# Pair plans of gate_up and down: four pairs in the last group, ten pairs in the second pass

## The chip, the core and the metric

The kernel runs on one core of one Trainium2 chip. The time is device microseconds of one execution. The kernel before takes 1428.76 us, the median of three runs (1428.35 to 1428.78).

## The reference

One layer of an encoder with a sequence of 256 rows, model width 2048 and a feed-forward width of 5632, all in float32:

```python
for l in range(DEPTH):
    h = rms_norm(x, norm_g[l, 0])
    ...
    x = x + mix @ w_out[l]
    x = x + cross_attention(rms_norm(x, norm_g[l, 1]), mem_n, w_xq[l], w_xkv[l], w_xo[l])
    x = x + swiglu(rms_norm(x, norm_g[l, 2]), w_gate_up[l], w_down[l])
return rms_norm(x, final_norm_g)

def swiglu(h, w_gate_up, w_down):
    gate, up = jnp.split(h @ w_gate_up, 2, axis=-1)
    return (jax.nn.silu(gate) * up) @ w_down
```

The change concerns only swiglu: the product with w_gate_up (2048 x 11264) and the product with w_down (5632 x 2048).

## The kernel before

**Split precision.** Each float32 operand is kept as two parts, hi and lo. ScalarE casts the weight (`wh`), VectorE subtracts (`wl = raw - wh`). A product of a 128-wide activation tile with a weight of 512 columns is three matmuls (`part`, L472 to L474): hi with wh, hi with wl, lo with wh.

**The weight stream.** The weights lie in DRAM in the order of their use, in slabs of 128 x 2048 (1 MB). `_load` fetches a slab into a raw buffer on SP's queue. `_plain` and `_sums` split its parts into a ring of wh/wl buffers; a part is split only when the ring has room, some three to four parts ahead of TensorE. There are three raw buffers, and a fourth one (`rx`) during gate_up; the ring loses one place (`wz`) and the fourth raw buffer within the last gate_up group, where `begin` calls `back`.

**Plain slabs and pairs.** A slab holds four blocks of 512 columns, for two tiles of the inner dimension and two column groups. In a plain slab (`N` in a plan) each block meets both row halves: 8 products, 24 matmuls, two parts of 1024 columns. A pair slab computes the same 2 x 2 x 2 block product with seven products (a scheme of the Strassen-Winograd kind), 21 matmuls. It uses sums of weight blocks and sums of activations. Its four parts are: products 1 and b0 (1024 columns), a0 (512), 5 and 7 (1024), 6 and a1 (1024). The sums of weights are either made by VectorE, with four adds of 512 columns, or partly by DMA: then a spare tile `t` (one of the residual buffers `res`) is filled with one block on SP's queue, ScalarE copies it, and GpSimd's queue adds two more blocks by an accumulating DMA; VectorE then makes only two adds, and the third part is split from `t`. Slabs of that kind are in `SUMMED`, and `_load` starts their sums three slabs ahead (`AHEAD`).

**Activations of a pair.** `combine` forms the sums of two activation tiles on VectorE and ScalarE: two adds of 256, four of 128, and the splits of the results into a `y` tile (`z` in gate_up) and, for a last quarter called x4, back into the first activation tile. The generator `combined` runs it, driven by a background queue and forced by `before` when a pair needs it. Each pass of down reuses the combined tiles that the pass before has made.

**Order.** gate_up has a first plain group and ten paired groups of eight slabs, nine with the plan `NSSNSSNN` and the last with `NSNSNSNN`. Its results go transposed through DRAM (`hidden`) and come back through `fetch` into the activation tiles f[0] to f[43]: f[20] to f[27] lie in the tiles `z` that hold gate_up's combined activations, f[28] to f[43] in those of gate_up's input. Down then runs in two passes of 22 slabs, each for 1024 output columns, with 6 pairs in the first pass and 9 in the second; the last 12 steps of the second pass are held back for `down_end`. In `paired_rows` the products go to PSUM banks: a0, a1, b0, b1 of the plain slabs to one pool of four (`pg` in the first pass of down, `pm` in the second), 1, 6, 7 and 5 of the pairs to the other. `mixed` and `done` add them to the residual when a pass is through its pairs, or through all; so the second pass's 1, 6, 7, 5 take, in this order, the banks that a0, a1, b0, b1 of the first pass had. The residual was stored to DRAM before gate_up and is read back after it into `res`.

The order on an engine follows the order of the program's list within gate_up and down (`last` in `_half`, `keep_place`) for splits and fetches, and a planner's placing for the rest.

Of the kernel before, what the change touches and what calls it, by code (L numbers as in the profile page):

```python
# [19 lines left out]
ALU = mybir.AluOpType  # L20
# [8 lines left out]
FT = DFF // P  # L29
# [10 lines left out]
ROWS = ((0, 512), (704, 1024), (1088, NBLK))  # L40

LATE = 12

GATE_UP = 1920 // 16 + 8
GROUPS = *["NSSNSSNN"] * 9, "NSNSNSNN"

DOWN = GATE_UP + 80
PASSES = "NNNNNSNNSNNSNSNNSNNSNN", "NSNSNSNSNSNSNSNSNSNNNN"

PAIRED = {a + i for a, plan in [(GATE_UP + 8 * j, GROUPS[j % len(GROUPS)]) for j in range(10)] + [(DOWN, PASSES[0]), (DOWN + 22, PASSES[1])]  # L50
          for i, x in enumerate(plan) if x in "Ss"}
AHEAD = (-3, -3)

SUMS = [{GATE_UP + 8 * j + i + a: GATE_UP + 8 * j + i for j in range(10) for i, x in enumerate(GROUPS[j % len(GROUPS)]) if x == "S"}
        for a in AHEAD]

SUMMED = {GATE_UP + 8 * j + i for j in range(10) for i, x in enumerate(GROUPS[j % len(GROUPS)]) if x == "S"}

LAG, OWED, SOON, FAR = 1.3, 0.9, 0.01, 18.0
V_NG = 0  # L60
# [16 lines left out]
class Stream:  # L77


    def __init__(self, tc, pools, W, bg):  # L80
        self.tc, self.nc, self.W, self.bg = tc, tc.nc, W, bg
        self.rawp, self.wp = pools
        self.order = []
        self.n = self.made = 0
        self.after = []
        self.halves = []
        self.at = self.phase = 0
        self.raw = None
        self.ring = [[self.wp, -1] for _ in range(3)]
        self.last = {}  # L90
        self.raws = [[self.rawp, -1] for _ in range(3)]
        self.sums = []
        self.places = []
        self.two = []
        self.begun = []

    def _buffers(self, n, m):

# [6 lines left out]
    def _load(self, n):  # L105

        nc = self.nc
        slot = min(self.raws, key=lambda x: x[1])
        slot[1] = n
        self.raw = slot[0].tile([P, 2048], F32, name="raw", tag="raw")  # L110
        if n // 16 in SUMS[0]:
            t = self.sums[0]
            self.sums.append(self.sums.pop(0))
            nc.sync.dma_start(t[:, 0:512], self.W[SUMS[0][n // 16]][:, 1536:2048])
            self.begun.append(t)
        if n // 16 in SUMS[1]:
            t = self.begun.pop(0)
            mark = len(nc.cur_bb.bb.instructions)
            nc.scalar.copy(t[:, 512:1024], t[:, 0:512])  # L119
            self.keep(mark)  # L120
            nc.gpsimd.dma_start(t, self.W[SUMS[1][n // 16]][:, 512:1536], accum_op=ALU.add)  # L121
            self.two.append(t)
        if n // 16 in SUMMED:
            nc.sync.dma_start(self.raw[:, 0:1536], self.W[n // 16][:, 0:1536])
            return
        for a, b in zip(CUTS[n], CUTS[n][1:]) if n in CUTS else [(0, 1024), (1024, 2048)] if self.after else [(0, 2048)]:
            (nc.scalar if (n, a) == (0, 0) else nc.sync).dma_start(self.raw[:, a:b], self.W[n // 16][:, a:b])
            if self.after:
                self.after.pop(0)()

    def _half(self):
# [161 lines left out]
class Block:  # L293
# [563 lines left out]
    def whole(self, c):  # L857
        return self.res[c].rearrange("p k r -> p (k r)")

    def leave(self, c):  # L860
        self.nc.sync.dma_start(self.rd[:, c * 1024:(c + 1) * 1024], self.whole(c))

# [237 lines left out]
    def gate_up(self, gp, f, z):  # L1100

        nc = self.nc
        box, g, stored = {}, {}, []
# [36 lines left out]
        def fetch(k0, k1, ahead, pause, after=0, slow=False):  # L1140

            m = {}
            for k in range(k0, k1 + ahead):
                if k < k1:
                    while len(stored) <= k // 4:
                        yield
                    while after and self.bg.now < stored[k // 4] + after:
                        yield
                    m[k] = self.tmp()
                    mark = self.mark()  # L1150
                    self.load_turned(m[k], self.ff, k)
                    self.keep_place(mark)
                    if slow and k < k0 + ahead - 1:
                        yield
                if k >= k0 + ahead:
                    while k0 == 0 and k - ahead >= 20 and "free" not in box:
                        yield
                    mark = self.mark()
                    self.split(f[k - ahead], m.pop(k - ahead))
                    self.keep_place(mark)  # L1160
                    self.have = k - ahead + 1
                    yield pause
# [41 lines left out]
        self.st.raws.append([rx, -1])  # L1204
        gate(ps[0])
        up(0, ps[1])
        early = fetch(0, FT - 22, 2, 2.0, 12, True)
        self.bg.drain(comb)
        for j in range(1, DFF // 512):
            plan = GROUPS[(j - 1) % len(GROUPS)]  # L1210
            if j == 10:
                box["free"] = True
            turns = [i for i, x in enumerate(plan) if x == "N"][:3]
            if j == 10:
                rest = fetch(FT - 22, FT, 6, SOON, slow=True)

            def begin(i):

                if (j, i) == (10, 5):
                    self.st.back(self.wz, rx)  # L1220
                if i in turns:
                    next(early, None)
                if j == 10 and i > 2:
                    next(rest)

            upped(j, self.paired_rows("w_gate_up", [j * 512, DFF + j * 512], self.h3, sums[:8 - plan.count("N")], plan, mixed, gated,
                                      before=begin, swap=j % 2 == 0)[0])
        more.close()
        for c, x in enumerate(whole):
            nc.sync.dma_start(x, self.rd[:, c * 1024:(c + 1) * 1024])  # L1230
        for _ in early:
            pass
        self.fetch = self.bg.add(rest)
# [1 line left out]
    def down(self, f, sp):  # L1235
# [4 lines left out]
        nc, st = self.nc, self.st  # L1240
        ss = self.rp.tile([P, 24], F32, name="rc", tag="rc")
        self.gap(sp, 192)
        z = [sp.tile([P, 768], F32R, name=f"y{i}") for i in range(8)]
        u = sp.tile([P, 512], F32, name="u")
        sums = [((2 * i, 2 * i + 1), z[i % 8]) for i in range(PASSES[1].count("S"))]
        made, split = [], []

        def combined(n):
            for ks, x in sums[len(made):n]:
                yield from self.combine(x, *(f[k] for k in ks))  # L1250
                made.append(x)
                yield 2.0
# [32 lines left out]
        asked = itertools.count(1)  # L1285

        def ready(k):

            need = min(FT, max(k + 3, FT - 22 + next(asked) * 3 // 4))
            while self.have < need:  # L1290
                self.bg.step(next(e for e in self.bg.q if e[0] is self.fetch))

        for i, plan in enumerate(PASSES):
            n = plan.count("S")
            g = self.bg.add(combined(n))
            late = (0, LATE)[i]
            plan = plan[:22 - late // 4]

            def before(j):
                while plan[j] == "S" and len(made) <= plan[:j].count("S"):  # L1300
                    self.bg.step(next(e for e in self.bg.q if e[0] is g))
                if late and j == len(plan) - 2:
                    st.back(self.wy)

            ps, rest = self.paired_rows("w_down", [2 * i * 512, (2 * i + 1) * 512], f, sums[:n], plan,
                                        lambda *q: mixed(2 * i, *q), lambda *q: done(2 * i, *q), ready, late, before, i == 1,
                                        () if i else range(2 * n, 2 * n + 8))
            if i == 0:
                done(1, *ps)
        return ss, ps, rest, split  # L1310
# [316 lines left out]
class Gla:  # L1627
# [364 lines left out]
```

## Time and profile before

| what | value |
|---|---|
| median of three runs | 1428.76 us |
| the profiled execution | 1428.43 us |
| its span, first to last instruction | 1426.6 us |
| ScalarE busy | 850.2 us (60%) |
| GpSimd busy | 243.4 us (17%) |
| HBM read / written | 321.07 MB / 22.54 MB |
| DMA queue of the hardware (q1), share of 16 engines | 57.4% |
| DMA queue of the software (q0, GpSimd) | 17.2% |

In the lines of the profile PE is TensorE, PEld its weight loads, DVE VectorE, ACT ScalarE, POOL GpSimd and SP the queue that issues most DMAs. A timeline row has the start and the length in microseconds, engine, line of the code, operation, output<-inputs, shape and count; in brackets stands how long the engine was idle before it, and what ended the wait. Lengths of instructions on one engine can overlap, so the distance between starts is also needed. A row by windows gives for each engine the busy time and the number of instructions in a stretch.

### The profile page before, as it was taken

To read this page: it belongs to the slowest core of one execution; us is meant where nothing else is said; L and a number is where in the kernel's file an instruction comes from. 1 tells how busy PE (TensorE), PEld (TensorE's weight loads), DVE (VectorE), ACT (ScalarE), POOL (GpSimd) and SP (SyncE) were. 2 spreads that over 40 slices of the span, in tenths; PEclk is the share of its full clock that TensorE was granted. 3 is DMA by queue.
4 is the path that set the end of the run, shared out by engine and by line. 5 is a ranking of instruction groups with operands and counts; after the bars stand their busy time and mean duration, and the time that the engine had idled before them with its cause. 6 is when DMAs were issued, how large, how long until landed. Compare 5 with 4: busy or idle time off the path is not lost.

```text
span 1426.6 us, 18663 instructions
## 1 busy us (share of the span) xinstructions
PE 1416.5 (99%) x6562; PEld 1176.1 (82%) x6562; DVE 1174.3 (82%) x1782; ACT 850.2 (60%) x1242; POOL 243.4 (17%) x315
## 2 busy tenths in 40 slices
PE   9999999999999999999999999999999999999997
PEld 8888888888888888888888888888888888788886
DVE  6667868787878767677578999999999988989997
ACT  7566665445755555555465676667666665655655
POOL 0000100003212233531331121122211024000000
PEclk9999999999999999999999999999999999999999
DMA  9886554457566797965798999999999898665554
GB/s 356 294 291 250 204 198 174 161 177 232 183 216 215 234 278 249 276 197 188 252 298 257 265 280 283 288 291 260 278 291 273 276 276 242 212 235 179 193 220 148
DMA packets 72462, 344.84 MB, mean 242 GB/s; under 512 B 10894, under 2 KB 12591, under 8 KB 45745
## 3 DMA queue, kind: packets, MB, share of 16 engines
q1 hardware_dynamic: 52976, 285.31, 57.4%
q0 software_dynamic: 18960, 57.69, 17.2%
q8 instruction: 51, 0.84, 0.2%
q10 hardware_dynamic: 432, 0.66, 0.1%
q14 instruction: 43, 0.34, 0.1%
HBM read 321.07 MB, written 22.54 MB: 241 GB/s over the span
## 4 chain that ended last, share of the span: by engine, by line
PE 92%; issue 3%; DVE 2%; DMA 2%; POOL 1%; ACT 0%; SPq 0%; DVEq 0%; ACTq 0%; POOLq 0%
PE pg L472 21%; PE pg L474 21%; PE pg L473 21%; PE pm L473 6%; PE pm L474 6%; PE pm L472 6%; PE pg L420 4%; PE pg L421 2%; PE pm L1445 1%; DMA raw<-in_W 1%; PE pm L1074 1%; DMA tmp<-hidden 1%; POOL tmp L605 1%; PE pm L1045 1%; DVE wl L179 0%
## 5 line engine op out<-in xcount | busy, mean ns | idle before, releaser
L167 DVE TENSOR_TENSOR wl<-raw,wh 128x1024 fp32r<-128x1024 f32 (+1 forms) x395 | 473.7, 1212 | 161.3 <-ACT wh L166 159.4
L166 ACT CAST wh<-raw 128x1024 fp32r<-128x1024 f32 (+1 forms) x395 | 406.4, 1042 | 253.0 <-PE pg L474 189.0
L472 PE MATMUL pg<-wh,act 128*128 128x512 f32 (+1 forms) x1165 | 455.5, 391 | 0.0
L474 PE MATMUL pg<-wh,act 128*128 128x512 f32 (+1 forms) x1165 | 453.9, 390 | 0.5 <-DVE act L322 0.5
L473 PE MATMUL pg<-wl,act 128*128 128x512 f32 (+1 forms) x1165 | 453.6, 389 | 0.2 <-DVE wl L167 0.2
L474 PEld LDWEIGHTS pg<-wh,act 128*128 128x128 f32 x1165 | 218.9, 188 | 47.0 <-DVE act L322 1.1
L472 PEld LDWEIGHTS pg<-wh,act 128*128 128x128 f32 x1165 | 219.0, 188 | 46.8 <-issue 1.5
L473 PEld LDWEIGHTS pg<-wl,act 128*128 128x128 f32 x1165 | 219.0, 188 | 45.1 <-DVE wl L167 0.5
L178 ACT CAST wh<-raw 128x1024 fp32r<-128x1024 f32 (+1 forms) x177 | 161.5, 918 | 158.8 <-DVE raw L189 62.7
L179 DVE TENSOR_TENSOR wl<-raw,wh 128x1024 fp32r<-128x1024 f32 (+1 forms) x177 | 182.7, 1057 | 25.7 <-ACT wh L178 24.3
L473 PE MATMUL pm<-wl,act 128*128 128x512 f32 x290 | 112.9, 389 | 0.2 <-DVE wl L167 0.2
L472 PE MATMUL pm<-wh,act 128*128 128x512 f32 x290 | 112.8, 389 | 0.0
L474 PE MATMUL pm<-wh,act 128*128 128x512 f32 x290 | 112.8, 389 | 0.0
L420 PE MATMUL pg<-act,wh 128*128 128x512 f32 x256 | 90.5, 395 | 0.0
L121 POOL DMA_DIRECT2D res<-in_W x39 | 35.0, 897 | 238.3 <-ACT res L119 211.1
L421 PE MATMUL pg<-act,wl 128*128 128x256 f32 x256 | 71.8, 280 | 0.0
L189 DVE TENSOR_TENSOR raw<-raw 128x512 f32<-128x512 f32 x99 | 68.2, 689 | 1.6
L473 PEld LDWEIGHTS pm<-wl,act 128*128 128x128 f32 x290 | 54.4, 188 | 11.8 <-DVE wl L167 0.5
L474 PEld LDWEIGHTS pm<-wh,act 128*128 128x128 f32 x290 | 54.4, 188 | 11.3
L472 PEld LDWEIGHTS pm<-wh,act 128*128 128x128 f32 x290 | 54.4, 188 | 11.3
L420 PEld LDWEIGHTS pg<-act,wh 128*128 128x128 f32 x256 | 48.1, 188 | 10.5
L178 ACT CAST wh<-res 128x1024 fp32r<-128x1024 f32 x39 | 41.2, 1055 | 14.8 <-PE pg L474 4.1
(376 smaller groups left out, 1933.0 us busy)
## 6 DMA issues: line engine op xcount, KB each, us to landing
raw<-in_W SPq DMA_DIRECT2D x207, 1024.0 KB, 5.5
raw<-in_W SPq DMA_DIRECT2D x39, 768.0 KB, 8.9
res<-in_W POOLq DMA_DIRECT2D x39, 512.0 KB, 9.7
res<-in_W SPq DMA_DIRECT2D x39, 256.0 KB, 4.9
raw<-in_W SPq DMA_DIRECT2D x11, 512.0 KB, 7.1
hidden<-g POOLq DMA_DIRECT2D x22, 256.0 KB, 4.0
tmp<-hidden POOLq DMA_DIRECT2D x44, 128.0 KB, 10.5
features<-tmp POOLq DMA_DIRECT2D x32, 128.0 KB, 4.6
```

Of the source, the lines that this page charges most:

```text
L121: nc.gpsimd.dma_start(t, self.W[SUMS[1][n // 16]][:, 512:1536], accum_op=ALU.add)
L166: nc.scalar.copy(wh[:, a:b], r[:, a:b])
L167: nc.vector.tensor_tensor(out=wl[:, a:b], in0=r[:, a:b], in1=wh[:, a:b].bitcast(F32), op=ALU.subtract)
L178: nc.scalar.copy(wh, src)
L179: nc.vector.tensor_tensor(out=wl, in0=src, in1=wh.bitcast(F32), op=ALU.subtract)
L189: nc.vector.tensor_tensor(out=out, in0=a, in1=b, op=ALU.add)
L420: self.nc.tensor.matmul(p[:, :], wh, slot[:, :], start=start, stop=False)
L421: self.nc.tensor.matmul(p[:, 0:R], wl, slot[:, 0:R], start=False, stop=stop)
L472: self.nc.tensor.matmul(p, hi, wh, start=start, stop=False)
L473: self.nc.tensor.matmul(p, hi, wl, start=False, stop=False)
L474: self.nc.tensor.matmul(p, lo, wh, start=False, stop=stop)
L605: self.nc.gpsimd.dma_start(t.rearrange("p (g t) -> p g t", t=32), src)
```

## The change

The plans are changed. `S` now stands for a pair with DMA sums and `s` for one whose sums VectorE makes. All ten paired groups of gate_up have four `S`. Down's first pass has its six pairs in the same places, as `s`. The second pass has ten pairs in place of nine; the first two slabs are both pairs, `S`, and the other eight are `s`. The sums of these two use residual tiles 2 and 3, so only tiles 0 and 1 are read back after gate_up, and 2 and 3 within the second pass. `begins` computes when a DMA sum is started (three slabs ahead, as before). `before` in `down` forces the combined activations of a pair one slab earlier than before, and `combined` waits where a `y` tile is still to be read. As the last gate_up group now uses all four tiles `z`, only f[0] to f[19] are fetched during gate_up, not f[0] to f[21], and `back` is called one slab later.

```diff
+EARLY = 20
-GROUPS = *["NSSNSSNN"] * 9, "NSNSNSNN"
+GROUPS = "NSSNSSNN",
-PASSES = "NNNNNSNNSNNSNSNNSNNSNN", "NSNSNSNSNSNSNSNSNSNNNN"
+PASSES = "NNNNNsNNsNNsNsNNsNNsNN", "SSNsNsNsNsNsNsNsNsNNNN"
+PLANS = [(GATE_UP + 8 * j, GROUPS[j % len(GROUPS)]) for j in range(10)] + [(DOWN, PASSES[0]), (DOWN + 22, PASSES[1])]
+PAIRED, SUMMED = ({a + i for a, plan in PLANS for i, x in enumerate(plan) if x in kinds} for kinds in ("Ss", "S"))
+def begins():
+    at = {}
+    for ns, tiles in (([n for n in sorted(SUMMED) if n < DOWN], 4), ([n for n in sorted(SUMMED) if n >= DOWN], 2)):
+        for i, n in enumerate(ns):
+            a = max(n - 3, ns[i - tiles] + 1) if i >= tiles else n - 3
+            at[a] = n
+    return at
+SUMS = begins()
...
-        if n // 16 in SUMS[0]:
+        if n // 16 in SUMS:
             t = self.sums[0]
             self.sums.append(self.sums.pop(0))
-            nc.sync.dma_start(t[:, 0:512], self.W[SUMS[0][n // 16]][:, 1536:2048])
-            self.begun.append(t)
-        if n // 16 in SUMS[1]:
-            t = self.begun.pop(0)
+            nc.sync.dma_start(t[:, 0:512], self.W[SUMS[n // 16]][:, 1536:2048])
             mark = len(nc.cur_bb.bb.instructions)
             nc.scalar.copy(t[:, 512:1024], t[:, 0:512])
             self.keep(mark)
-            nc.gpsimd.dma_start(t, self.W[SUMS[1][n // 16]][:, 512:1536], accum_op=ALU.add)
+            nc.gpsimd.dma_start(t, self.W[SUMS[n // 16]][:, 512:1536], accum_op=ALU.add)
...
+    def fetch_rows(self, cs):
+        for c in cs:
+            self.nc.sync.dma_start(self.whole(c), self.rd[:, c * 1024:(c + 1) * 1024])
...
-                    while k0 == 0 and k - ahead >= 20 and "free" not in box:
-                        yield
...
-        early = fetch(0, FT - 22, 2, 2.0, 12, True)
+        early = fetch(0, EARLY, 2, 2.0, 12, True)
...
-                rest = fetch(FT - 22, FT, 6, SOON, slow=True)
+                rest = fetch(EARLY, FT, 6, SOON, slow=True)
...
-                if (j, i) == (10, 5):
+                if (j, i) == (10, 6):
                     self.st.back(self.wz, rx)
...
-        for c, x in enumerate(whole):
-            nc.sync.dma_start(x, self.rd[:, c * 1024:(c + 1) * 1024])
+        self.fetch_rows((0, 1))
+        self.st.sums = whole[2:]
...
-        sums = [((2 * i, 2 * i + 1), z[i % 8]) for i in range(PASSES[1].count("S"))]
-        made, split = [], []
+        sums = [((2 * i, 2 * i + 1), z[i % 8]) for i in range(sum(x in "Ss" for x in PASSES[1]))]
+        made, split, past = [], [], [0]
         def combined(n):
             for ks, x in sums[len(made):n]:
+                while len(made) - past[-1] > 7:
+                    yield
                 yield from self.combine(x, *(f[k] for k in ks))
...
-            need = min(FT, max(k + 3, FT - 22 + next(asked) * 3 // 4))
+            need = min(FT, max(k + 3, EARLY + next(asked) * 3 // 4))
...
             def before(j):
-                while plan[j] == "S" and len(made) <= plan[:j].count("S"):
+                past.append(sum(x in "Ss" for x in plan[:j]))
+                while len(made) < sum(x in "Ss" for x in plan[:j + 2]):
                     self.bg.step(next(e for e in self.bg.q if e[0] is g))
+                if i and j == plan.rindex("S") + 2:
+                    self.fetch_rows((2, 3))
```

More of the change, by code (lines that the diff above doesn't have):

```diff
@@ L42 @@
 LATE = 12
+EARLY = 20
 GATE_UP = 1920 // 16 + 8
-GROUPS = *["NSSNSSNN"] * 9, "NSNSNSNN"
+GROUPS = "NSSNSSNN",
 DOWN = GATE_UP + 80
-PASSES = "NNNNNSNNSNNSNSNNSNNSNN", "NSNSNSNSNSNSNSNSNSNNNN"
[L50 to L57, printed above, removed]
+PASSES = "NNNNNsNNsNNsNsNNsNNsNN", "SSNsNsNsNsNsNsNsNsNNNN"
[6 more added lines that the diff above has]
+            a = max(n - 3, ns[i - tiles] + 1) if i >= tiles else n - 3
+            assert a not in at and a < n, (a, n)
+            at[a] = n
+    return at
+SUMS = begins()
 LAG, OWED, SOON, FAR = 1.3, 0.9, 0.01, 18.0
@@ L94, in __init__ @@
         self.two = []
-        self.begun = []
     def _buffers(self, n, m):
@@ L1210, in gate_up @@
             plan = GROUPS[(j - 1) % len(GROUPS)]
-            if j == 10:
-                box["free"] = True
             turns = [i for i, x in enumerate(plan) if x == "N"][:3]
             if j == 10:
-                rest = fetch(FT - 22, FT, 6, SOON, slow=True)
+                rest = fetch(EARLY, FT, 6, SOON, slow=True)
             def begin(i):
-                if (j, i) == (10, 5):
+                if (j, i) == (10, 6):
                     self.st.back(self.wz, rx)
@@ L1293, in down @@
         for i, plan in enumerate(PASSES):
-            n = plan.count("S")
+            n = sum(x in "Ss" for x in plan)
             g = self.bg.add(combined(n))
@@ L1306, in down @@
                                         lambda *q: mixed(2 * i, *q), lambda *q: done(2 * i, *q), ready, late, before, i == 1,
-                                        () if i else range(2 * n, 2 * n + 8))
+                                        () if i else range(2 * n, EARLY))
             if i == 0:
```

## The prediction

> **What bounds the kernel now.** I read the page first: busy times, granted clock and the chain that ended last.
>
> ```profile
> span 1426.6 us, 18663 instructions
> PE 1416.5 (99%) x6562; PEld 1176.1 (82%) x6562; DVE 1174.3 (82%) x1782; ACT 850.2 (60%) x1242; POOL 243.4 (17%) x315
> PEclk9999999999999999999999999999999999999999
> PE 92%; issue 3%; DVE 2%; DMA 2%; POOL 1%; ACT 0%; SPq 0%; DVEq 0%; ACTq 0%; POOLq 0%
> ```
>
> TensorE works all the time at full clock and is 92% of the chain. Its busy time can hide small pauses, since a matmul is shown as 0.39 us long although the next starts earlier. The starts tell the real pace, so next I read the timeline of TensorE, in the stretches that the change touches.
>
> ```profile
> 1140.18 0.39 PE L472 MATMUL pg<-wh,act 128*128 128x512 f32 x1
> 1157.18 0.39 PE L472 MATMUL pm<-wh,act 128*128 128x512 f32 x1
> ...
> 1214.98 0.48 PE L472 MATMUL pg<-wh,act 128*128 128x512 f32 x1
> 1215.71 0.47 PE L472 MATMUL pm<-wh,y 128*128 128x512 f32 x1 [0.25 <-ACT y L338]
> ...
> 1231.46 0.39 PE L474 MATMUL pg<-wh,act 128*128 128x512 f32 x1
> 1232.33 0.50 PE L474 MATMUL pg<-wh,act 128*128 128x512 f32 x1 [0.48 <-DVE act L322]
> ```
>
> The first two rows are 75 matmuls apart: 17.00 / 75 = 0.2267 us for each. That is the price of a matmul of 512 columns here, not 0.39. The other two pairs of rows are pauses: 0.73 and 0.87 us from start to start in place of 0.227, so 0.50 + 0.64 = 1.14 us lost. Both stand in down's first pass, and both wait for the combined activations of a pair (y, and the quarter of x4 that is written back into act). Last, the engines by stage: the last gate_up group, down's first pass, down's second pass.
>
> ```profile
> 1150.00:1200.00 50.00, 50.00 (x222) 41.41 (x221) 40.98 (x50) 28.19 (x35) 16.01 (x20) 1.00 0.85 256
> 1186.40:1303.40 117.00, 116.27 (x511) 95.55 (x510) 106.51 (x176) 68.41 (x101) 16.45 (x19) 1.00 0.66 215
> 1303.40:1404.60 101.20, 100.99 (x445) 82.93 (x445) 97.00 (x140) 60.17 (x77) 0.00 (x0) 1.00 0.55 201
> ```
>
> The columns are span, PE, PEld, DVE, ACT, POOL, clock, DMA share, GB/s. VectorE is busy 82%, 91% and 96% of the three. So TensorE sets the time, and VectorE, which splits every weight, is close behind it in down.
>
> **Removed matmuls.** Two more pairs, one in the last gate_up group and one in down's second pass. A pair slab has 7 products of 3 matmuls, a plain one 8 of 3: 3 matmuls each, 6 in all, 6 x 0.2267 = 1.36 us. They lie on the path throughout. (The Trainium skill, "TensorE: Matmul & The Clock Gate", section Back-to-back issue gap, gives about 131 ns per matmul of 512 columns for a stream of weight loads and matmuls; by that the six would be worth 0.79 us. The rows here show 227 ns, and the sum goes by them.)
>
> **Combined activations a slab earlier.** This moves no work, only its place in VectorE's and ScalarE's queues, some 5 us ahead of the pair. The two pauses should go: 1.14 us. Bounds: 0 (VectorE is full there and merely makes the weights late instead) to 1.14. I take 1.0. Two activation rows (20 and 21) are no longer fetched in the last gate_up group but in the first pass: two 256-wide splits, 0.67 us of VectorE by the rows of the next part. Those are hidden behind the fetches' lead of several steps; without that cover they cost 0.67.
>
> **Fourth pair of the last group.** VectorE gets, for a DMA-summed pair, three 1024-wide splits, one of 512 and two adds of 512, in place of two splits of 1024. The rows that price it are these, of the join of down's two passes, where VectorE runs without a gap:
>
> ```profile
> 1289.14 1.23 DVE L179 TENSOR_TENSOR wl<-raw,wh 128x1024 fp32r<-128x1024 f32 x1 [1.30 <-ACT wh L178]
> 1290.28 0.68 DVE L322 TENSOR_TENSOR res<-res,u 128x512 f32<-128x512 f32 x1
> 1290.88 3.49 DVE L167 TENSOR_TENSOR wl<-raw,wh 128x1024 fp32r<-128x1024 f32 x3
> 1294.29 0.68 DVE L322 TENSOR_TENSOR u<-u,pm 128x512 f32<-128x512 f32 x1
> 1294.89 0.68 DVE L322 TENSOR_TENSOR res<-res,pg 128x512 f32<-128x512 f32 x1
> 1295.48 0.74 DVE L322 TENSOR_TENSOR tmp<-u,pm 128x256 f32<-128x256 f32 x2
> 1296.15 0.42 DVE L322 TENSOR_TENSOR res<-res,tmp 128x256 f32<-128x256 f32 x1
> ...
> 1304.49 1.28 DVE L322 TENSOR_TENSOR res<-res,pg 128x512 f32<-128x512 f32 x2
> ...
> 1308.77 0.28 DVE L322 TENSOR_TENSOR tmp<-tmp 128x128 f32<-128x128 f32 x1
> 1308.97 0.69 DVE L189 TENSOR_TENSOR raw<-raw 128x512 f32<-128x512 f32 x1
> ...
> 1312.05 2.36 DVE L167 TENSOR_TENSOR wl<-raw,wh 128x1024 fp32r<-128x1024 f32 x2
> ```
>
> From start to start a 1024-wide split takes (1294.29 - 1290.88) / 3 = 1.137 us, a 512-wide operation 0.60 (1294.29 to 1294.89), one of 256 0.335 (two in 0.67), one of 128 0.20. So the DMA-summed pair is 3 x 1.137 + 3 x 0.60 = 5.2 us of VectorE, a plain slab 2.27, a pair with all four sums on VectorE 6.4. The extra pair adds 2.9 us to a stretch of 50 where VectorE is free for 9.0 (the first window row); the other groups carry four pairs each. I cost it at 0; if VectorE were full there, 2.9.
>
> **The new start of the second pass.** Here is the loss that I expect. The two pairs now come right behind the join, where VectorE must also add all of pass one into the residual. Its row of 1289.14 waited 1.30 for ScalarE, so it has caught up by then; from 1290.28 it never waits. In the changed program's order, its queue from there to the second res<-res,pg holds six 1024-wide splits (plain slabs 20 and 21, and two parts of the first pair), eleven operations of 512 and eight of 256: 6.82 + 6.60 + 2.68 = 16.1 us, so 1306.4. What waits for it on TensorE:
>
> ```profile
> 1303.45 0.39 PE L472 MATMUL pm<-wh,f 128*128 128x512 f32 x1
> 1313.65 0.39 PE L472 MATMUL pm<-wh,z 128*128 128x512 f32 x1
> ```
>
> The second pass starts at 1303.45. Its first pair's product 5 comes nine matmuls later, 1305.49, and takes the PSUM bank (b1 of pass one) that this very add frees: 0.9 us late. Next in the queue come the rest of that pair (1.137), the second pair's first two parts, its two adds and one 256-wide activation add (1.137 + 0.60 + 0.60 + 0.335 + 0.60), then its third part (1.137): 1311.95. The changed program, which starts some matmuls with wh before those with wl, first needs that at matmul 33, 1303.45 + 33 x 0.2267 = 1310.93: 1.0 late. With one more 256, the fourth part and the next plain slab it is 1314.56, wanted at matmul 44, 1313.43: 1.1 late. The latest counts, not their sum. Before, the same plain slab was split from 1312.05 on, and its first matmul started at 1313.65, so nothing was late. I add 0.2 for a ScalarE cast that now precedes the copy of u: 1.3 us. Bounds: 0 (as in the gate_up groups, where two such pairs stand side by side at full pace) to 2.9 (all of a pair's extra VectorE work).
>
> **DMA.** The two sums and two residual rows are asked for on queues that are otherwise free:
>
> ```profile
> raw<-in_W SPq DMA_DIRECT2D x207, 1024.0 KB, 5.5
> res<-in_W POOLq DMA_DIRECT2D x39, 512.0 KB, 9.7
> ```
>
> GpSimd's accumulation lands 9.7 us after issue. ScalarE's copy ahead of it stands three slabs, some 15 us, before the pair, which covers it. In SP's queue the loads of residual rows 2 and 3 wait for the two pairs' third parts; the weight loads behind them wait anyway for raw buffers that are freed by the same pairs' fourth parts. Both 0; uncovered, an accumulation would cost up to 9.7. The second pass's fourth combine, one more than before (2 x 0.335 + 4 x 0.20 + 0.335 + 2 x 0.20 = 2.2 us of VectorE) spreads over later slabs of a pass in which VectorE idles 4.2 us: 0, at worst 2.2.
>
> **Sum.** -1.36 - 1.0 + 1.3 = -1.06. Own time of the profiled execution: 1428.43 (its span 1426.6 and 1.8 around it), which lies 0.33 below the median of 1428.76. So 1428.43 - 1.06 = 1427.4 for such an execution and 1427.7 by the median.
>
> **Rivals.**
> 1. The join costs nothing: VectorE works further ahead than I counted, and matmuls are reordered around late halves. For it: side-by-side pairs at full pace in gate_up. Against it: the 16.1 us queue. 1428.76 - 1.36 - 1.14 = 1426.3.
> 2. Asking ahead does not do what it says: the two pauses come from a full VectorE (106.5 of 117) and only move. 1428.76 - 1.36 + 1.3 = 1428.7.
> 3. Slower: VectorE, once late at the join, cannot catch up in the second pass, because the fourth combine falls into the same slabs. Then the pair's 2.9, the combine's 2.2 and the two late fetch splits' 0.67 all end up as waits of TensorE: 5.8 - 1.36 = +4.4, 1433.2. It decides from the point where the 4.2 us that VectorE idles in the second pass no longer lie behind the combines. Against it: a pair with a plain slab takes TensorE 45 x 0.2267 = 10.2 us and VectorE 8.7 without a combine, so 1.5 are regained each time.
> 4. Each VectorE instruction holds its queue for its whole length (0.68 in place of 0.60). The 30-odd operations of the join then take 0.08 x 30 = 2.4 more: 1430.1. The starts above speak against it. (The Trainium skill, "VectorE: DVE Perf Modes", section The TRN2 errata, gives (N+151)/0.96 ns for such an add, 691 ns at 512: the length agrees, the spacing does not.)
>
> **How the numbers follow.** Forecast 0.53 (own range 1426.7 to 1428.8), rival 1 0.15, rival 2 0.16, rival 3 0.13, rival 4 0.03. What a measurement can tell from no change is 0.2%, 2.86 us: under 1425.9 or over 1431.6. Faster than that needs rival 1 and a little more: 0.05. Slower needs most of rival 3's price: 0.11. Within: 0.84. Range 1426.0 to 1430.5: it takes in rival 1, 2 and 4 and the low half of rival 3.
>
> **What would show it.** In the new trace 0.227 us from start to start without the two pauses at the y operands of pass one; a first pause of about 1 us at the first product 5 of the second pass, behind res<-res,pg, and a few tenths at the second pair; VectorE without a gap from the last pair of pass one on; matmuls of the last group at full pace. I am wrong if that start has no pause, if pauses recur at later pairs, or if TensorE waits for an accumulation.

## The result, and the profile after

The changed kernel takes 1431.80 us, the median of 14 runs (1430.50 to 1433.16), against 1428.77 of the kernel before in the same rounds. The ratio is 1.0021 (95% interval 1.0013 to 1.0029): it is slower by about 3 us. Its profiled execution took 1431.15 us, against 1428.43.

The page of the changed kernel, with span, busy times and the chain that ended last:

```profile
span 1429.0 us, 18704 instructions
PE 1416.4 (99%) x6556; PEld 1175.0 (82%) x6556; DVE 1180.3 (83%) x1797; ACT 854.7 (60%) x1252; POOL 246.4 (17%) x318
PE 89%; DVE 3%; issue 3%; DMA 2%; POOL 1%; ACT 1%; SPq 0%; ACTq 0%; DVEq 0%; POOLq 0%
```

Six matmuls are gone (6562 to 6556), yet TensorE's share of the chain fell from 92% to 89%. The whole page hides what happened; the stages do not. The engines by stage, for the last gate_up group, down's first pass and its second pass, with the columns that the prediction explains:

```profile
1149.20:1199.20 50.00, 50.00 (x222) 41.40 (x222) 43.43 (x53) 29.66 (x37) 16.25 (x20) 1.00 0.84 263
1186.00:1304.20 118.20, 116.42 (x511) 95.34 (x510) 106.95 (x178) 69.27 (x105) 20.02 (x23) 1.00 0.70 218
1304.20:1407.10 102.90, 101.51 (x443) 82.39 (x441) 100.70 (x151) 62.92 (x83) 0.00 (x0) 1.00 0.59 212
```

The last group still runs at 222 matmuls in 50 us, with VectorE at 43.43 in place of 40.98. The passes grew, to 118.2 and 102.9 us from 117.0 and 101.2, although the second pass has three matmuls fewer (the rows show two fewer, since this window ends one matmul later). The timeline of TensorE shows where, first in pass one:

```profile
1215.20 0.39 PE L477 MATMUL pm<-wh,y 128*128 128x512 f32 x1
1215.43 0.39 PE L478 MATMUL pm<-wl,y 128*128 128x512 f32 x1
...
1231.02 0.49 PE L477 MATMUL pm<-wh,y 128*128 128x512 f32 x1
1233.27 0.50 PE L478 MATMUL pm<-wl,y 128*128 128x512 f32 x1 [1.76 <-DVE wl L184]
1233.61 0.39 PE L479 MATMUL pm<-wh,y 128*128 128x512 f32 x1
```

The pause at the first pair's y operands (0.73 before) is gone. The second pair, slab 8 of pass one, pauses from 1231.02 to 1233.27, 2.25 us, and now waits for a split of the weights instead of activations. Then the start of pass two:

```profile
1306.27 0.61 PE L477 MATMUL pg<-wh,y 128*128 128x512 f32 x2
1307.03 0.50 PE L477 MATMUL pm<-wh,act 128*128 128x512 f32 x1
1307.37 0.39 PE L478 MATMUL pg<-wl,y 128*128 128x512 f32 x1
...
1311.47 0.61 PE L477 MATMUL pg<-wh,y 128*128 128x512 f32 x2
1313.17 0.50 PE L477 MATMUL pg<-wh,y 128*128 128x512 f32 x1 [1.08 <-ACT wh L183]
1313.51 0.40 PE L478 MATMUL pg<-wl,y 128*128 128x512 f32 x1
```

A row with x2 holds two matmuls, the second 0.23 later. So there are four late starts, of 0.53, 0.34, 1.47 and 0.34 us in place of 0.227 each: 1.77 us lost. The loss of a stretch is summed in this way in the rest of the text, over all starts that come more than 0.24 us after the one before. By it pass one loses 2.52 us (before: 1.35) and the second pass 1.77 (before: 0) until its last slabs.

The account of the profiled executions closes: 0.46 less before down starts (the three matmuls of the last group, 0.68, and 0.2 more earlier on), then from down's first matmul to its last 234.57 us against 231.98, +2.59 = -0.68 + 1.17 + 1.77 + 0.3 at the end of down, and 0.6 behind the last matmul and around the span. -0.46 + 2.59 + 0.6 = 2.7. The first term belongs to one execution each: e4_pass9 and e7_plain_first, whose gate_up is that of the changed kernel, start down at 1187.29 and 1186.64 in place of 1185.96.

### The profile page after: what moved, and what is told of

The parts are those of the page before. It is cut to its first block, busy times and chain, and to the rows that moved or that the text cites. A ratio compares the mean times of both kernels' runs of the same rounds, so it can differ in the third digit from the quotient of the medians.

```text
span 1429.0 us, 18704 instructions
## 1 busy us (share of the span) xinstructions
PE 1416.4 (99%) x6556; PEld 1175.0 (82%) x6556; DVE 1180.3 (83%) x1797; ACT 854.7 (60%) x1252; POOL 246.4 (17%) x318
## 4 chain that ended last, share of the span: by engine, by line
PE 89%; DVE 3%; issue 3%; DMA 2%; POOL 1%; ACT 1%; SPq 0%; ACTq 0%; DVEq 0%; POOLq 0%
PE pg L477 20%; PE pg L479 20%; PE pg L478 20%; PE pm L478 6%; PE pm L479 6%; PE pm L477 6%; PE pg L425 4%; PE pg L426 2%; DMA raw<-in_W 1%; PE pm L1456 1%; DVE wl L184 1%; PE pm L1084 1%; DMA tmp<-hidden 1%; DVE wl L172 1%; POOL tmp L610 1%
## 5 line engine op out<-in xcount | busy, mean ns | idle before, releaser
L477 PE MATMUL pm<-wh,act 128*128 128x512 f32 x284 | 110.6, 389 | 0.1
L479 PE MATMUL pm<-wh,act 128*128 128x512 f32 x284 | 110.5, 389 | 0.0
L183 ACT CAST wh<-res 128x1024 fp32r<-128x1024 f32 x42 | 44.3, 1055 | 17.2 <-PE pg L479 6.3
```

The costliest lines, as they stand in the source:

```text
L183: nc.scalar.copy(wh, src)
L477: self.nc.tensor.matmul(p, hi, wh, start=start, stop=False)
L479: self.nc.tensor.matmul(p, lo, wh, start=False, stop=stop)
```

## The experiments

Two theories were set against each other first. Theory F: the two activation rows that are no longer fetched in the last gate_up group (f[20], f[21]) share the DMA engines with the raw load of slab 8 and make it late. Theory A: asking for the combined activations a slab ahead pushes the splits of the weights back on VectorE. Every experiment ran in five rounds beside the kernel before. Times are medians; "loss" is from the profiled execution, without what a slow clock adds (last section).

| kernel | us | before, us | ratio (95%) | loss, pass one | loss, pass two |
|---|---|---|---|---|---|
| before | 1428.77 | | | 1.35 | 0 |
| changed | 1431.80 | 1428.77 | 1.0021 (1.0013-1.0029) | 2.52 | 1.77 |
| e1_fetch20 | 1430.52 | 1428.86 | 1.0014 (1.0005-1.0023) | 3.0, and a slow clock | 0 |
| e2_ask | 1429.15 | 1428.86 | 1.0003 (0.9994-1.0011) | 1.35 | 0 |
| e3_group3 | 1430.53 | 1428.86 | 1.0012 (1.0003-1.0021) | 1.34 | 1.77 |
| e4_pass9 | 1429.45 | 1428.86 | 1.0007 (0.9999-1.0016) | 2.5, and a slow clock | 0 |
| e5_fetch22 | 1430.02 | 1429.17 | 1.0007 (0.9998-1.0016) | 1.1 | 1.77 |
| e6_both | 1430.06 | 1429.17 | 1.0007 (0.9998-1.0016) | 1.0 | 2.0 |
| e7_plain_first | 1431.95 | 1429.17 | 1.0023 (1.0014-1.0032) | 3.1 | 2.0 |
| e8_fetch18 | 1432.52 | 1429.17 | 1.0027 (1.0016-1.0037) | 3.1, and a slow clock | 0 |
| e9_plain_two | 1434.03 | 1428.99 | 1.0034 (1.0021-1.0048) | 1.4 | 0.2, and 4.4 at the end, and a slow clock |
| e10_nine | 1427.86 | 1428.99 | 0.9991 (0.9983-1.0000) | 1.1 | 0 |
| e11_sums_one | 1433.14 | 1428.99 | 1.0028 (1.0017-1.0040) | 1.5 | 0.2, and 4.9 at the end, and a slow clock |
| e12_spread | 1429.18 | 1428.91 | 1.0001 (0.9992-1.0010) | 1.1 | 1.6 |

At the end of down, another 0.5 to 1.0 us is lost in every kernel but e9_plain_two and e11_sums_one.

### One part of the change alone

**The fetches alone.** The kernel before, with f[20] and f[21] moved into pass one:

```diff
-        early = fetch(0, FT - 22, 2, 2.0, 12, True)
+        early = fetch(0, 20, 2, 2.0, 12, True)
...
-                rest = fetch(FT - 22, FT, 6, SOON, slow=True)
+                rest = fetch(20, FT, 6, SOON, slow=True)
...
-            need = min(FT, max(k + 3, FT - 22 + next(asked) * 3 // 4))
+            need = min(FT, max(k + 3, 20 + next(asked) * 3 // 4))
```

> The kernel before with one edit: activation rows 20 and 21 are fetched in down's first pass, not in the last gate_up group (22 fetches become 24 there). Theory F (the two extra fetches share the DMA engines with the weight load of the first pass's second pair, which then lands about 1.7 us later, and TensorE waits for its wl): a pause of 1 us or more at the second pair, 1.0 to 2.0 us above the kernel before. Theory A (the pause comes from asking for the combined activations a slab earlier, which pushes the weights' splits back on VectorE and ScalarE): the pauses stay those of before, time within 0.5 us of the kernel before.

By the ratio it is 2.0 us slower than before (0.7 to 3.3). The second pair of pass one pauses twice, for 1.09 and 1.58 us, and behind that matmuls start only every 0.427 us for a while (last section). Two fetches at this place are enough to make the kernel slower.

**Asking ahead alone.** The kernel before, with only this line changed:

```diff
-                while plan[j] == "S" and len(made) <= plan[:j].count("S"):
+                while len(made) < plan[:j + 2].count("S"):
```

> The kernel before with one edit: the combined activations of a pair are forced one slab earlier. Theory F: the two pauses of before (1.1 us) vanish and none comes in their place, 0.7 to 1.3 us below the kernel before. Theory A: a pause of 1 us or more at the first pass's second pair, on wl, 0 to 1.5 us above the kernel before.

It gains nothing (ratio 1.0003), and the loss of pass one is the same, 1.35. The timeline of this kernel shows why; what used to wait for activations at the first pair waits for weights at the second:

```profile
1231.49 0.39 PE L472 MATMUL pm<-wh,y 128*128 128x512 f32 x1
1232.40 0.50 PE L473 MATMUL pm<-wl,y 128*128 128x512 f32 x1 [0.52 <-DVE wl L179]
```

VectorE works in the order of the program's list and is busy 106.5 of 117 us in this pass, before as with this edit, so an operation that is put ahead pushes others back. Both theories missed in part: the gain that theory F expected did not come, and theory A's pause did, of 0.91 us.

### One part of the change undone

**The last group as before** (three pairs, f[20] and f[21] fetched in it):

```diff
-EARLY = 20
+EARLY = 22
-GROUPS = "NSSNSSNN",
+GROUPS = *["NSSNSSNN"] * 9, "NSNSNSNN"
...
+                    while k0 == 0 and k - ahead >= 20 and "free" not in box:
+                        yield
...
```

> The changed kernel with the last gate_up group as before: three pairs, 22 rows fetched in gate_up, buffers given back at slab 5. Theory F: no pause over 0.5 us in the first pass; against the changed kernel +0.68 for the matmuls and -2.2 for the pause, so about 1430.2 or 1.5 below it. Theory A: the pause at the second pair stays, and the time is 0.5 to 0.9 above the changed kernel. In both the second pass starts with 1.5 to 1.9 us of pauses.

The 2.25 us pause is gone, and pass one loses 1.34, as in e2_ask. The start of pass two loses the same 1.77 as in the changed kernel.

**The second pass as before** (nine pairs, all residual rows read back at once):

```diff
-PASSES = "NNNNNsNNsNNsNsNNsNNsNN", "SSNsNsNsNsNsNsNsNsNNNN"
+PASSES = "NNNNNsNNsNNsNsNNsNNsNN", "NsNsNsNsNsNsNsNsNsNNNN"
...
-        self.fetch_rows((0, 1))
-        self.st.sums = whole[2:]
+        self.fetch_rows(range(4))
...
```

> The changed kernel with the second pass as before: nine pairs after plain slabs, sums by VectorE, all residual rows read back after gate_up. If the loss at the start of the second pass is due to the two pairs side by side, its 1.5 to 1.9 us of pauses go and 0.68 us of matmuls come back: 0.8 to 1.2 below the changed kernel, about 1430.8. If the queue of the join is late anyway (through the activations asked ahead), pauses of 1 us or more stay there and the time is not below the changed kernel. The pause of the first pass stays either way.

The other half of the picture: no loss at the start of pass two, while the pause at slab 8 stays (1232.48 to 1234.74, 2.26 us). The time fell by more than the 0.8 to 1.2 us expected, by 2.0 us against the changed kernel by the ratios (1.0021 less 1.0007); its profiled execution, at 1431.72 us, was the slowest of its 11. Theory F's account of the pause stands so far, and the two losses are separate.

### Is it the fetches or the fourth pair?

In e3_group3 both went together. With four pairs all four tiles z are in use in the last group; but if its first pair takes z[0], that tile is free early, and f[20] and f[21] can be fetched there although the fourth pair stays:

```diff
-EARLY = 20
+EARLY = 22
...
+                    while k0 == 0 and k - ahead >= 20 and "free" not in box:
+                        yield
...
-        sums = [((2 * i, 2 * i + 1), z[(i + 1) % 4]) for i in range(4)]
+        sums = [((2 * i, 2 * i + 1), z[i]) for i in range(4)]
...
+                if (j, i) == (10, 4):
+                    box["free"] = True
+                if i in turns or (j, i) == (10, 5):
...
```

> The changed kernel, but activation rows 20 and 21 are fetched within the last gate_up group again, as before the change, although that group keeps its four pairs: gate_up's first pair takes tile z[0] instead of the last, so that z[0] is free after the second slab. Theory F (the two extra fetches delay the raw load of slab 8 of pass one): slab 8's load lands some 6.4 us after its issue instead of 8.1, the pause of 2.25 us at the second pair of pass one goes, and pass one loses about 1.3 as in the kernel that only asks ahead; the join of the passes still loses 1.8. Time 1428.8 - 1.36 + 1.8 = 1429.2, or 1429.2 to 1430.2. Rival G (the late load comes from the fourth pair of the last group, whose accumulation and whose later slabs push the weight loads back, and not from the fetches): the pause of 2 us stays, 1431.3 to 1431.8.

Theory F, not G. The first cast of slab 8's weights on ScalarE, in the kernel before, in the changed one and in e5_fetch22:

```profile
1222.93 1.05 ACT L178 CAST wh<-raw 128x1024 fp32r<-128x1024 f32 x1 [1.09 <-DMA raw<-in_W]
```

```profile
1224.28 1.05 ACT L183 CAST wh<-raw 128x1024 fp32r<-128x1024 f32 x1 [4.50 <-DMA raw<-in_W]
```

```profile
1223.05 1.05 ACT L183 CAST wh<-raw 128x1024 fp32r<-128x1024 f32 x1 [2.53 <-DVE tmp L327]
```

From the start of down these are 36.5, 38.3 and 36.4 us. In the changed kernel ScalarE had waited 4.50 us for the raw load. The last row names a VectorE operation as what ended the wait, but by the trace the last of the load's 16 parts had landed 0.10 us before this cast in all fourteen kernels, whatever the row names, so the load sets the cast's start in each. It starts 36.3 to 36.7 us after the start of down in the nine kernels without extra fetches in pass one, and 38.2 to 38.9 in the four with two (changed, e1_fetch20, e4_pass9, e7_plain_first). The chain of waits has that load, before and in the changed kernel:

```profile
1216.42 6.41 DMA raw<-in_W
```

```profile
1216.07 8.11 DMA raw<-in_W
1224.18 0.02 issue
1224.20 0.04 ACTq L183
1224.24 0.04 issue
1224.28 1.06 ACT wh L183
...
1232.08 1.15 DVE wl L184
1233.23 0.04 issue
1233.27 0.50 PE pm L478
```

And the DMA view of 30 us around it (1195 to 1225, and 1196 to 1226 in e5_fetch22) shows what ran beside it: the columns are packets, MB and share of 16 engines for the software queue. The changed kernel:

```profile
q0 software_dynamic: 912, 2.49, 40.0%
```

e5_fetch22; the kernel before has the same row in 1195.5 to 1225.5:

```profile
q0 software_dynamic: 816, 2.23, 33.8%
```

The two fetches are only 0.26 MB, but 6.2% of 16 engines for 30 us: 1.9 us of all DMA engines, 0.9 for each row of 128 KB. That is about how much later the cast comes. (The Trainium skill, "DMA: Bandwidth & Descriptors", section Queues, rings and completion order, says that a DMA engine takes turns, packet by packet, between the queues it has work for; by that the fetches on GpSimd's queue delay the load on SP's queue although neither waits for the other in the program. The rows agree.)

**More of them.** The kernel before with four rows, f[18] to f[21], moved into pass one (as e1_fetch20, with 18 for 20):

> The kernel before with four activation rows (18 to 21) instead of none moved from the last gate_up group to the first pass; two rows cost 1.7 us. Theory F by dose (each fetch keeps all DMA engines some 0.9 us longer from the raw load of slab 8): its landing another 1.7 us later, the pause at the second pair 4 us, time 1432 to 1433.5. Rival T (a threshold: the third and fourth fetch delay slab 8 no further, because they come after its load in the queues, or push only splits back): 1430.5 to 1431.5.

The time, 3.9 us over before by the ratio (2.3 to 5.3), is in theory F's range, but the way is not: the cast waits for the raw load only 2.40 us and comes 37.8 us after the start of down, and the chain to the pause runs through a landing of a fetch (6.55 us) as well. So the third and fourth fetch delay slab 8's load no further, which is rival T's condition, though its time (1430.5 to 1431.5) was passed. Nor do they show as dearer: the profiled executions of e1_fetch20 and this kernel, both with a slow clock, took 1431.76 and 1432.17 us and lost 3.0 and 3.1 in pass one, and the intervals of the ratios overlap.

### The start of the second pass

Put a plain slab first, and let two more pairs have DMA sums; once with the fetches repaired and once in the changed kernel with nothing else altered:

```diff
-"SSNsNsNsNsNsNsNsNsNNNN"
+"NSSNSSNsNsNsNsNsNsNNNN"
```

> The kernel e5_fetch22 with the second pass begun by a plain slab: NSSNSSNsNsNsNsNsNsNNNN, ten pairs as in the changed kernel, four of them with DMA sums from the two residual tiles. Theory: the pauses at the join (0.53, 0.34, 1.47, 0.34 at matmul starts) go, since the first pair's product 5 comes 24 matmuls (5.4 us) later and VectorE was at most 1.8 late; each DMA sum also takes two adds (1.2 us) off VectorE. Time 1428.8 - 1.36 = 1427.4 (1427.0 to 1428.2): faster than before. Rival J1 (the backlog only moves to the next side-by-side pairs): pauses of 1 to 2 us at slabs 4 and 5 of the second pass, 1428.5 to 1429.5. Rival J2 (an accumulation by DMA comes late, because a tile is free only one slab before its next use): one pause of over 2 us ended by the DMA of raw or of the residual tile.

> The changed kernel with nothing but the plan of its second pass altered, to NSSNSSNsNsNsNsNsNsNNNN (ten pairs, a plain slab first, four DMA sums). Theory (costs add: join 1.8, extra fetches 1.5 to 2): 1431.8 - 1.8 = 1430.0, with the pause of 2.25 us at the second pair of pass one still there and none over 0.3 us at the start of the second pass. Rival J1 (the join's loss only moves to slabs 4 and 5): 1431.3 to 1432.

Neither gained anything: e6_both is level with e5_fetch22, and e7_plain_first with the changed kernel. The join's loss fell from 1.77 to about 0.2, but the pass lost about 1.8 later on, most of it at its second two side-by-side pairs. ScalarE's timeline in e6_both suggests a reason; the third and fourth accumulation come late, as the two tiles are lent again right behind their first use:

```profile
1320.09 0.62 ACT L124 COPY res<-res 128x512 f32<-128x512 f32 x1 [2.20 <-DMA res<-in_W]
1320.61 0.62 ACT L183 CAST wh<-raw 128x512 fp32r<-128x512 f32 x1
...
1328.20 1.05 ACT L183 CAST wh<-res 128x1024 fp32r<-128x1024 f32 x1 [1.86 <-DMA res<-in_W]
```

Behind the first of these waits VectorE idled 1.51 us, and the pauses follow (0.53 and 1.14 us from start to start). The pauses are where rival J1 put them, at slabs 4 and 5; its time came true in e7_plain_first and was passed in e6_both (1430.06 for at most 1429.5). That the late accumulations, the cause of rival J2, made them is not shown: e12_spread below loses nearly as much at such pairs without them.

With the fetches repaired, DMA sums for the first two pairs only:

```diff
-"SSNsNsNsNsNsNsNsNsNNNN"
+"NSSNsNsNsNsNsNsNsNsNNN"
```

> The kernel e5_fetch22 (four pairs in the last gate_up group, rows 20 and 21 fetched there) with the second pass NSSNsNsNsNsNsNsNsNsNNN: ten pairs, one plain slab first, and only the first two pairs with DMA sums, for which both residual tiles are free early. In e6_both ScalarE waited 2.2 and 1.9 us for the accumulations of the third and fourth sum, so VectorE idled 1.5 and the pauses of 0.53 and 1.14 at slabs 4 and 5 followed. Theory (late accumulations made those pauses; the plain slab first had removed the join's loss): none of them is left, the second pass loses at most 0.5 at its start, time 1428.8 - 1.36 + 0.3 = 1427.7 (1427.2 to 1428.6). Rival V (VectorE is full in the second pass, 96 of 100 us; with eight s pairs of 5.2 to 6.4 us and four combines it falls behind again somewhere): pauses of 1 us or more spread over the later pairs, 1428.8 to 1430.

The start loses 0.2 and the pass nothing up to its last slabs, as expected; the time is the worst of all and lies in no expected range. To have ten pairs with only one side-by-side, the last pair must be the last slab before the twelve steps that are held back, and then the adds into the residual stand ahead of everything that the end needs. TensorE and ScalarE there:

```profile
1403.96 0.39 PE L479 MATMUL pm<-wh,act 128*128 128x512 f32 x1
1407.21 0.79 PE L477 MATMUL pm<-held,act 128*128 128x512 f32 x1 [2.85 <-ACT held L162]
```

```profile
1406.54 0.62 ACT L162 CAST held<-raw 128x512 fp32r<-128x512 f32 x1 [5.55 <-DVE res L327]
```

A pause of 3.24 us: not less VectorE work, but VectorE work moved to a place without cover. The same kernel with DMA sums also for the last four pairs of pass one (`"NNNNNsNNsNNSNSNNSNNSNN"`):

> The kernel e9_plain_two with DMA sums also for the last four of the six pairs of pass one (slabs 11, 13, 16, 19 as S). Each takes two adds of 512 (1.2 us) off VectorE, which is busy 107 of 117 us in pass one. Theory (pass one's pauses come from VectorE): the pauses around slab 11 (about 0.5 us at 1249 to 1251 us) go, those at slab 8 stay; time 0.4 to 0.6 below e9_plain_two. Rival D (accumulations come late as in e6_both, each over a tile that the pair before has just left): ScalarE waits for DMA of res at one of those slabs, a pause of 0.5 to 2 us, 0.5 to 2 above e9_plain_two.

0.9 us below e9_plain_two by the medians, with overlapping intervals. VectorE's busy time in pass one fell from 106 to 101 us, yet pass one's loss did not (1.5 against 1.4): slab 11 still pauses, 0.66 us from start to start, for a split wl. Rival D did not show either; ScalarE waited for no accumulation in that pass. Inconclusive as to the time; that fewer adds on VectorE remove pass one's pauses got no support.

**Ten pairs, spread.** A plain slab first, one after the last pair, and the third and fourth DMA sum six slabs behind the first two:

```diff
-"SSNsNsNsNsNsNsNsNsNNNN"
+"NSSNsNsNSSNsNsNsNsNNNN"
```

> The kernel e5_fetch22 with the second pass NSSNsNsNSSNsNsNsNsNNNN: ten pairs, a plain slab first, a plain slab after the last pair, and four DMA sums of which the third and fourth come six slabs after the first two, so that their residual tiles have long been free. In e9_plain_two nothing was lost from slab 3 to slab 18; its 3.2 us went at the end, where the held weights' cast on ScalarE waited for VectorE's adds into the residual, since its last pair was the last slab before the held ones. Theory: the start loses 0.2 as there, the side-by-side pairs at slabs 8 and 9 nothing, the end is as in the kernel with nine pairs: 0.68 - 0.2 = 0.5 below e10_nine's 1427.9, so 1427.4 (1427.0 to 1428.0). Rival V (VectorE cannot carry ten pairs in that pass; the side-by-side pairs in its middle fall behind with the combines of pairs seven to ten): pauses of 0.5 to 1.5 us after slab 8, 1428.2 to 1429.5.

Rival V. Start and end are as expected, no accumulation is late, and the side-by-side pairs in the middle pause for VectorE's splits:

```profile
1348.20 0.50 PE L478 MATMUL pg<-wl,y 128*128 128x512 f32 x1 [0.25 <-DVE wl L184]
...
1352.81 0.50 PE L478 MATMUL pg<-wl,y 128*128 128x512 f32 x1 [0.66 <-DVE wl L184]
```

**Nine pairs.** What is left when the second pass is as before and the fetches are repaired (e5_fetch22 with e4_pass9's edit):

> The kernel e5_fetch22 with the second pass as before the change (NsNsNsNsNsNsNsNsNsNNNN, nine pairs, all residual rows read back after gate_up). What is left of the change is the fourth pair of the last gate_up group and the earlier combined activations. Theory (costs add): no pause at the start of the second pass, pass one as in the kernel that only asks ahead, so 1428.8 - 0.68 = 1428.1 (1427.7 to 1428.9). Rival: the fourth pair costs what it saves somewhere else, 1428.8 to 1429.5.

1427.86 us, ratio 0.9991 (0.9983 to 1.0000): that agrees with a fourth pair worth its three matmuls (0.68) and 0.27 less lost in pass one, and this version is below both kernels, if only just. Its waits of TensorE in all of down are two:

```profile
PE pm L478 <- DVE wl L172: 0.3, 1, 0.3
PE pm L478 <- DVE wl L184: 0.2, 1, 0.2
```

## Why the prediction was wrong

The forecast was -1.06 us, the profiled executions show +2.72. Of the 3.8 between them 1.0 is the term for asking ahead, 1.2 the fetches that were priced at 0, and 0.5 the start of the second pass; the other 1.1 lies before down (0.2), at its end (0.3) and behind its last matmul and around the span (0.6), and its cause stays open.

**Removed matmuls, -1.36: right.** 6562 became 6556, and the last group's three show as 402.56 to 401.88 us from gate_up's first z operand to the start of down.

**Combined activations a slab earlier, -1.0: this step failed.** The prediction named 0 as the bound, "VectorE is full there and merely makes the weights late instead", and chose nearly the other end. e2_ask shows the bound: the loss stays at 1.35. The evidence stood in the prediction's own window row, VectorE busy 106.5 of 117 us, together with the program's fixed order on that engine. Rival 2 was right here.

**The two fetch rows, 0, at worst 0.67: this step failed most.** They were priced by VectorE's splits alone, with the fetches' lead as cover. Their DMA was not priced, although the step moved it into the stretch where slab 8's load runs. They cost 1.2 us in the changed kernel's profile (2.52 against e2_ask's 1.35), and 2.0 by the ratios of the changed kernel and e5_fetch22 (1.0021 less 1.0007), whose intervals overlap; the granted clocks point to a slower clock in part of the executions for that difference (last section).

**The start of the second pass, +1.3: right place, too small, and only in part for the reason given.** It measured 1.77, the same in e3_group3 and e5_fetch22, and 0 in e4_pass9 and e10_nine, where the second pass is undone. The prediction let product 5 wait for the bank that res<-res,pg frees. It did not: its first matmul (1306.27) started on time, nine matmuls behind the pass's first at 1304.23, and before that add began. What came late were the fourth parts of both pairs, with ScalarE's casts of them, and the second pair's third part. ScalarE and VectorE in the changed kernel, at the second pair:

```profile
1312.07 1.05 ACT L183 CAST wh<-raw 128x1024 fp32r<-128x1024 f32 x1 [2.06 <-DVE raw L194]
```

```profile
1306.87 0.68 DVE L327 TENSOR_TENSOR res<-res,pg 128x512 f32<-128x512 f32 x1
1307.47 2.95 DVE L184 TENSOR_TENSOR wl<-raw,wh 128x1024 fp32r<-128x1024 f32 x3
1310.34 0.68 DVE L194 TENSOR_TENSOR raw<-res,raw 128x512 f32<-128x512 f32 x1
1310.94 0.42 DVE L327 TENSOR_TENSOR tmp<-f 128x256 f32<-128x256 f32 x1
1311.28 0.68 DVE L194 TENSOR_TENSOR raw<-raw 128x512 f32<-128x512 f32 x1
1311.88 1.22 DVE L184 TENSOR_TENSOR wl<-res,wh 128x1024 fp32r<-128x1024 f32 x1
```

The second add ends at 1311.96, 7.73 us after the pass's start; the prediction's queue had 7.4, so VectorE was counted well. But behind the add comes a cast of 1.05 us, which the prediction left out, and the program wants this cast's product 6 ahead of the third part's wl, so TensorE goes on only at 1313.17. That wl, the last row, ends at 1313.10, 0.02 before the cast, so by these rows TensorE would have waited nearly as long without the cast: this pause is the third part that the prediction called 1.0 late, and it cost 1.35 with the start behind it. The other 0.42 fell at the first pair's fourth part, a wait that the prediction does not list.

**Fourth pair of the last group, 0, and the accumulations, 0: right.** 222 matmuls in 50 us, and no wait for an accumulation at the join of the changed kernel. e6_both shows the second without cover: 1.9 to 2.2 us of ScalarE's waiting, not the bound of 9.7.

**Rival 3** (slower, VectorE cannot catch up in the second pass) had the sign and came nearest in size (+4.4), but not the mechanism: the changed kernel's later pairs do not pause. Yet e12_spread fits its idea of a VectorE that cannot carry ten pairs: it cured the join and lost 1.4 us for VectorE's splits later in that pass. Rival 1 fell with the 1.77 us lost at the join. Nothing supports rival 4: the add of 1306.87 is followed by the next start at 1307.47, 0.60 later.

## What to carry to other kernels

Price each moved instruction on every resource that it uses: a fetch of 128 KB cost little on VectorE and 0.9 us of all DMA engines, in front of a load with no slack. With VectorE 91% busy in a fixed order, putting work ahead on it only changed which wait was seen, and a tenth pair cost more than it saved in each of the places tried. When two engines alternate on a chain (add, cast, matmul), follow the chain through both, not the longer queue alone.

## What the runs showed of the hardware

A short pause can cost more than itself. In e4_pass9 the pause at slab 8 was 2.26 us long, as in the changed kernel (2.25). Its timeline behind the pause:

```profile
1234.74 0.50 PE L478 MATMUL pm<-wl,y 128*128 128x512 f32 x1 [1.75 <-DVE wl L184]
...
1235.81 0.63 PE L478 MATMUL pm<-wl,y 128*128 128x512 f32 x1
1236.23 0.63 PE L479 MATMUL pm<-wh,y 128*128 128x512 f32 x1
```

From start to start these are 0.427 us in place of 0.227, for some eight matmuls: 1.6 us more. The engines in two stretches of 4 us, across the pause and behind it, with the granted clock third from the end; first e4_pass9, then the changed kernel:

```profile
1231.00:1235.00 4.00, 2.10 (x8) 1.20 (x8) 4.00 (x10) 3.57 (x6) 0.00 (x0) 1.00 0.00 0
1235.00:1239.00 4.00, 4.00 (x12) 3.09 (x12) 4.00 (x6) 2.38 (x3) 0.00 (x0) 0.57 0.45 129
```

```profile
1230.00:1234.00 4.00, 2.22 (x9) 1.33 (x8) 4.00 (x9) 3.95 (x6) 0.00 (x0) 1.00 0.00 0
1234.00:1238.00 4.00, 4.00 (x19) 3.09 (x18) 4.00 (x5) 3.45 (x6) 0.00 (x0) 1.00 0.58 184
```

One lost the clock and the other did not. The same drop followed the pauses of e1_fetch20, e8_fetch18 and, after 3.24 us, e9_plain_two and e11_sums_one; the changed kernel and e7_plain_first passed through theirs at full clock in the execution that was profiled. (The Trainium skill, "TensorE: Matmul & The Clock Gate", Part 1: The HAM clock gate, says that the clock is halved after an idle window of about 3.4 us, and that the windows run freely; by that it would depend on where a pause falls. That the same pause has it or not agrees, and if the clock was halved, a mean of 0.57 over 4 us is 3.4 us of it; but here TensorE was idle for little over 2 us, less than a whole window.) How often it happens can be judged by the granted clock of each run, a mean over the whole execution with three decimals. In the seven kernels with a pause of over 2 us, or two close pauses that add up to it, 22 of 65 runs had 0.997 or less; in the six other changed versions 1 of 66, and in the kernel before 1 of 93. In e7_plain_first the four runs at 0.996 to 0.997 are the four slowest, 1432.78 to 1434.75 us, and the seven others took 1431.30 to 1432.04.
